# Splitting the weights of a two-layer trunk into high and low parts: units of 512 or of 1024 columns

## The chip, the cores and the metric

The kernel runs on one core of one Trainium2 chip. The metric is the device time of one execution in microseconds. The engines are named as in the profile: PE is the tensor engine's matrix product, PEld its weight load, DVE the vector engine, ACT the scalar engine, POOL the general engine, SP the engine that issues nearly all transfers. L55 is line 55 of the kernel before. The change keeps the line numbers, so L55 is the same statement in both.

## The reference

A trunk of two layers is applied to 288 tokens (256 of a prompt and 8 samples of 4) with 1024 features, all in float32. Each layer is

```python
h = h + 0.5 * swiglu(rmsnorm(h, ...), ffn1_gate_up, ffn1_down)
h = h + mixer(rmsnorm(h, ...))           # layer 0: Mamba-2, layer 1: RWKV-7
h = h + 0.5 * swiglu(rmsnorm(h, ...), ffn2_gate_up, ffn2_down)
h = h + (p[i] @ ple_in[i]) * sigmoid(rmsnorm(h, ...) @ ple_gate[i])
```

and a last norm follows. The feed-forward width is 22 x 128 = 2816. Besides the output, the mixers' new states are returned (the Mamba states and convolution rows, the RWKV states and shifted rows).

## The kernel before, in words

Features lie on the 128 partitions and the 288 tokens are the columns, so that a product takes a weight tile of 128 x 128 as the stationary operand and an activation tile of 128 x 288 as the moving one. The stages follow one another in this order: feed-forward, Mamba, feed-forward, the part with p ("ple"), feed-forward, RWKV, feed-forward, ple, final norm.

**Precision.** Most products are made in float32r, a format that the tensor engine takes in one pass. To keep float32's accuracy a weight w is split into a rounded high part and the exact rest, and so is the activation x; `mm3` (L144 to L149) then adds three products into one bank: high x high (L147), high x low (L148) and low x high (L149).

**The stream of weights.** `Stream` (L26) holds the tiles in the order of use: 3016 tiles in 377 units of UT = 8 tiles. `load` (L37 to L42) issues one transfer of 512 KB for a unit on SP's queue, into one of four raw buffers. `ahead` (L44 to L59) splits pieces of PT tiles: ACT copies the piece to a float32r buffer `whi` (L55), then DVE subtracts that from the raw piece into `wlo` (L56). `next` (L61) returns the two parts of the next tile, after it has called `ahead` with `la_split` = 16 tiles and `la_units` = 4 units:

```python
while self.split < min(self.n, self.used + tiles_split):
    ...
    src = self.raw[self.split // UT][:, (self.split % UT) * P:(self.split % UT + PT) * P]
    hi = self.k.wsp.tile([P, PT * P], F32R, tag="whi", name=f"whi{i}")
    lo = self.k.wsp.tile([P, PT * P], F32R, tag="wlo", name=f"wlo{i}")
    nc.scalar.activation(hi, src, AF.Copy)
    nc.vector.tensor_tensor(lo, src, hi.bitcast(F32), ALU.subtract)
    ...
    self.split += PT
```

The pool `wsp` (L1682) has eight buffers of each of `whi` and `wlo`, of 4 tiles each: 32 tiles. A buffer can be written again when the products of all its tiles have been made. A raw buffer can be loaded again when all of its tiles have been split. Part of RWKV's weights (88 tiles, the stream `wn`) is used whole, in float32, and is never split.

**What sets the order.** Each engine works through its own queue in order, and an instruction that waits holds up all that stand behind it on that engine. The program is written in Python without an explicit order for the queues: a planner (the tile framework's scheduler) places the instructions on each engine by the order in which the program makes them, by their readiness and by its own estimates of how long each takes. So the splits stand in ACT's and DVE's queues among the other work of those engines, at places that the planner chose:

- in a feed-forward part (`ffn_in`, L299) the gates' evacuation and the split of the hidden values; at its end `h_done` (L343), which makes the next operand from h and adds to the next norm's sum;
- in Mamba (`mamba`, L838) the split operands for the first projections (L853 and the lines after it), the convolutions (L671), the step sizes, the states;
- in RWKV (`rwkv`) the mixed operands (`mix`, L1100), the short products and copies of the recurrence for each pair of heads (`prep`, `chain`), and at the end the products with w_o, whose last operand hangs on the last pair's group norm;
- in the prologue (L424 to L434) the first operands, made tile by tile with calls of `ahead(min(PT * k, la_split), la_units)` between them, then the squares for the first norm.

The products themselves stand in PE's queue in an order that the planner chose likewise.

Of the kernel before, what the change touches and what calls it, by code (L numbers as in the profile page):

```python
# [19 lines left out]
UT = 8  # L20
PT = 4
# [4 lines left out]
class Stream:  # L26
    """Weight tiles [128, 128] in the order of use: loaded in units of UT tiles, split in
    pieces of PT tiles into a float32r high part and the exact float32r rest, or left whole."""
# [40 lines left out]
    def next_whole(self, name, kt, mt):  # L69
        """The next tile as float32, for a product in the tensor engine's own four passes."""  # L70
        self.order.append((name, kt, mt))
        while self.loaded < min(self.n, self.used + 2 * UT):
            self.load()
        u, o = divmod(self.used, UT)
        self.used += 1
        return self.raw[u][:, o * P:(o + 1) * P]


class K:
# [44 lines left out]
    def after(self, later, earlier):  # L124
        """Queue later behind earlier on their engine."""
# [3 lines left out]
    def act(self, out, in_, func, bias=None, scale=None):  # L129
        """An activation. Those of one table set stay together in the engine's queue, behind the set's load."""  # L130
# [20 lines left out]
    def hilo(self, hi, lo, src, scale=None):  # L151
        """hi = float32r(src * scale), lo = src * scale - hi, exactly."""
# [19 lines left out]
    def rsqrt(self, out, ps, eps, shift_eps=True, n=NT, y=None):  # L172
        """out = 1/sqrt(ps + eps): exp(-ln/2), then a Newton step."""
# [10 lines left out]
    def rstd(self):  # L184
        """The mean square's matrix product and the reciprocal root, on all partitions."""
# [23 lines left out]
    def renew(self, lo, hi, dt=F32R):  # L209
        """The shared tiles lo to hi anew, for values of type dt."""  # L210
# [29 lines left out]
    def ffn(self, name, down_next, ple=None, early=None):  # L240
        """The feed-forward part, and the part with p where it comes next: its layer, what comes after,
        whether p's products were made early; the layer of p's products where they fill the wait for
        the next norm: they are kept in DRAM."""
# [38 lines left out]
    def p_load(self, i, tiles):  # L282
        """The split parts of p for layer i."""
# [15 lines left out]
    def ffn_in(self, name, down_next, mid=None):  # L299
        """h += 0.5 * swiglu(x): x's split parts are in xh, xl (without the row's 1/rms)."""  # L300
# [44 lines left out]
    def h_done(self, mo, g):  # L345
        """A tile of h is final: its part of the next norm's sum and of the next operand."""
        if g is not None:
            self.split_h(mo, g)
        self.stat_add(mo)
# [37 lines left out]
    def final_done(self, mo):  # L387
        """A tile of h is final: its part of the norm's sum, the tile times the norm's weights."""
# [9 lines left out]
    def final(self, pool):  # L398
        """The norm and the output with the tokens on the partitions; the last block ends with the samples."""
# [24 lines left out]
    def prologue(self, g):  # L424
        """The split parts of the first operand; products that bring the tensor engine to its full clock."""
# [53 lines left out]
class Mamba:  # L479
# [65 lines left out]
    # dt and everything that only hangs on it, for all heads  # L545
# [26 lines left out]
    def dt_tokens(self):  # L572
        """dt, dt*A and their sums with the tokens on the partitions; the samples' three times."""
# [45 lines left out]
    def bc(self, ps, h, cols):  # L619
        """The running sums of the pair of heads from h, on 64 partitions each."""  # L620
# [5 lines left out]
    def exps(self, g):  # L626
        """exp(a_i - a_j), 0 where j > i, for the group's four heads; exp(a_i) for its two pairs."""
# [18 lines left out]
    def conv(self, g, n, ct, ps, raw):  # L646
        """The conv's rows to keep, the conv itself (without silu); raw: ps lacks the row's 1/rms."""
# [34 lines left out]
    def silus(self, g, conv, z):  # L682
        """The silus of group g's conv channels and of the gates z."""
# [8 lines left out]
    def ssd(self, g):  # L692
# [5 lines left out]
        # token-major x and B  # L698
# [37 lines left out]
        # (C_i . B_j), masked  # L736
# [7 lines left out]
        # the prompt's states  # L744
# [66 lines left out]
    def norm_act(self, g):  # L811
        """w = 1/sqrt of the group's mean square / 2, and (2 w)^2."""
# [7 lines left out]
    def norm_dve(self, g):  # L820
        """A Newton step, -1/sqrt = (v (2 w)^2 - 3) w, and the next operand."""
# [15 lines left out]
def mamba(k, gain, g_next):  # L837
# [9 lines left out]
    with k.tc.tile_pool(name="mamba", bufs=1) as pool:  # L847
# [20 lines left out]
        def boundary(g):  # L868
            """Between the tiles of group g and those of the next; the exponentials of two groups at once."""
# [122 lines left out]
class Rwkv:  # L992
# [49 lines left out]
    def lead(self, g, r):  # L1042
        """u, the shifted difference, the mixed operands; the first halves of the small products."""
# [29 lines left out]
    def gates(self):  # L1073
        """The first half of the gate's small products."""
# [15 lines left out]
    def stack(self, out, src, rows, other):  # L1090
        """The split parts on two ranges of partitions."""
# [3 lines left out]
    def stacked(self, ps, w, x, n, rows, start=True):  # L1095
        """A product whose operand's parts are stacked on n partitions, the high ones on rows; w twice there."""
# [3 lines left out]
    def mix(self, i, kt, out):  # L1100
        """The mixed operand i: float32, or in split parts (of r and v; the second half of v's where xx was)."""
# [13 lines left out]
    def sigmoid(self, out, ps, bias):  # L1115
        """exp(-ln(1 + exp(-z))), z = ps + bias kept from where exp leaves ln's range (there it is under 1e-18)."""
# [6 lines left out]
    def proj(self, n, i, x, p):  # L1123
        """A projection k, v or r of a pair of heads."""
# [15 lines left out]
    def bulk(self, p):  # L1140
        """The projections of a pair of heads that prep needs: decay and a (small), k, r."""
# [17 lines left out]
    def bulk2(self, p):  # L1159
        """The others: g, v, and v by tokens."""  # L1160
# [437 lines left out]
def _tiles(w):  # L1598
    """[K, M] -> [kt, mt, 128, 128], zero-padded."""
    kt, mt = -(-w.shape[0] // P), -(-w.shape[1] // P)  # L1600
    if w.shape != (kt * P, mt * P):
        z = np.zeros((kt * P, mt * P), w.dtype)
        z[:w.shape[0], :w.shape[1]] = w
        w = z
# [140 lines left out]
```

## Time and profile before

| | |
|---|---|
| median of 3 runs (range) | 1566.1 us (1565.0 to 1567.6) |
| profiled execution: span from first to last instruction | 1563.5 us |
| profiled execution: its own time beside the span | none is listed; the runs' median is 2.6 us above the span |
| PE busy | 1547.2 us, 99% |
| PEld busy | 1435.2 us, 92% |
| DVE busy | 1102.7 us, 71% |
| ACT busy | 982.5 us, 63% |
| the high parts, L55 on ACT | 754 instructions of 128 x 512, 472.0 us |
| the low parts, L56 on DVE | 754 instructions of 128 x 512, 516.0 us |
| raw weights, L40 on SP | 377 transfers of 512 KB |
| mean granted clock of the tensor engine | 0.997 |

In a group's row the numbers behind the bar are its busy time in us and the mean of one instruction in ns; then comes the idle time of the engine ahead of it, with what ended most of that. A row of waits reads "engine, instruction <- what it waited for: us in all, times, longest". In a row of a timeline stand start, duration, engine, line, operation and operands. Matmuls overlap in the pipeline: the mean of one is longer than the time from one start to the next.

### The profile page before, as it was taken

What the parts mean: (1) busy time and instruction counts of PE and PEld (TensorE: products, weight loads), DVE (VectorE), ACT (ScalarE), POOL (GpSimd) and SP (SyncE); (2) the same over time, 40 slices, a digit from 0 to 9 for tenths busy, and PEclk for the clock granted to TensorE, in tenths of its full rate; (3) what the DMA queues carried; (4) which work ended last, traced back from release to release, by engine and by line L of the source; (5) the groups of instructions that cost most, each with busy time, mean ns of one, the idle gap of its engine ahead of it and who ended that gap; (6) DMA issues with size and microseconds to landing.
All of it is one profiled execution on the core that took longest, in us unless ns stands there. A gap on an engine that the chain in (4) does not pass through costs nothing. (4 is left out here: it accounts for less than half of the span.)

```text
span 1563.5 us, 35166 instructions
## 1 busy us (share of the span) xinstructions
PE 1547.2 (99%) x13954; PEld 1435.2 (92%) x13954; DVE 1102.7 (71%) x2321; ACT 982.5 (63%) x2241; POOL 46.9 (3%) x142
## 2 busy tenths in 40 slices
PE   9999999999999999999999999999999999999998
PEld 9999998998989999999999999677777778999997
DVE  7666678888888666656866655976666777766656
ACT  7555458999987555545755555776666755555545
POOL 0000002111100000000000000100000000000000
PEclk9999999999999999999999999999999999999999
DMA  7555564765765555555555555432221224555551
GB/s 250 163 164 170 166 197 141 251 203 200 246 208 184 178 163 167 170 162 164 169 172 165 163 169 169 147 97 70 71 78 50 62 60 133 185 162 168 169 165 58
DMA packets 75572, 243.44 MB, mean 156 GB/s; under 512 B 11728, under 2 KB 16976, under 8 KB 75408
## 3 DMA queue, kind: packets, MB, share of 16 engines
q1 hardware_dynamic: 75408, 241.21, 49.4%
q8 instruction: 109, 1.79, 0.5%
q14 instruction: 55, 0.45, 0.1%
HBM read 226.54 MB, written 14.64 MB: 154 GB/s over the span
## 5 line engine op out<-in xcount | busy, mean ns | idle before, releaser
L147 PE MATMUL bank<-act,whi 128*128 128x288 f32 x2760 | 825.6, 300 | 5.8 <-ACT act L138 4.2
L148 PE MATMUL bank<-act,whi 128*128 128x288 f32 x2760 | 819.0, 297 | 0.9 <-DVE act L156 0.7
L149 PE MATMUL bank<-act,wlo 128*128 128x288 f32 x2760 | 814.3, 295 | 0.1
L55 ACT ACTIVATE whi<-raw 128x512 fp32r<-128x512 f32 x754 | 472.0, 631 | 434.4 <-PE bank L148 421.1
L56 DVE TENSOR_TENSOR wlo<-raw,whi 128x512 fp32r<-128x512 f32 x754 | 516.0, 690 | 263.3 <-ACT whi L55 235.2
L148 PEld LDWEIGHTS bank<-act,whi 128*128 128x128 f32 x2760 | 521.4, 189 | 10.2 <-issue 4.2
L147 PEld LDWEIGHTS bank<-act,whi 128*128 128x128 f32 x2760 | 517.0, 188 | 14.7 <-ACT act L138 5.4
L149 PEld LDWEIGHTS bank<-act,wlo 128*128 128x128 f32 x2760 | 520.5, 189 | 3.7 <-issue 0.8
L147 PE MATMUL bank<-more,whi 128*128 128x288 f32 x192 | 56.7, 295 | 0.0
L148 PE MATMUL bank<-more,whi 128*128 128x288 f32 x192 | 56.4, 294 | 0.0
L149 PE MATMUL bank<-more,wlo 128*128 128x288 f32 x192 | 56.4, 294 | 0.0
L321 DVE TENSOR_TENSOR t<-bank,rstd 128x288 f32<-128x288 f32 x88 | 39.9, 457 | 22.9 <-PE bank L149 22.9
L324 DVE TENSOR_TENSOR u<-bank,s 128x288 f32<-128x288 f32 x88 | 39.8, 457 | 22.6 <-PE bank L149 22.6
L671 DVE SCALAR_TENSOR_TENSOR conv_a<-X,vec,conv_a 128x312 f32<-128x312 f32 x96 | 51.1, 536 | 2.6 <-ACT conv_a L138 2.2
L138 ACT ACTIVATE s<-t 128x288 f32<-128x288 f32 x104 | 45.8, 443 | 6.1 <-DVE t L366 3.5
L138 ACT ACTIVATE X<-bank 128x256 f32<-128x256 f32 (+2 forms) x98 | 30.7, 340 | 20.0 <-PE bank L1304 19.2
L1131 PE MATMUL bank<-act,raw 128*128 128x288 f32 x128 | 42.5, 439 | 0.0
L138 ACT ACTIVATE act<-h,vec 128x288 fp32r<-128x288 f32 (+1 forms) x71 | 37.1, 528 | 7.3 <-DMA h<-in_xT 2.7
L148 PEld LDWEIGHTS bank<-more,whi 128*128 128x128 f32 x192 | 36.3, 189 | 0.0
L149 PEld LDWEIGHTS bank<-more,wlo 128*128 128x128 f32 x192 | 36.2, 189 | 0.0
L147 PEld LDWEIGHTS bank<-more,whi 128*128 128x128 f32 x192 | 36.0, 187 | 0.0
L133 ACT ACT_TABLE_LOAD x25 | 32.1, 1283 | 1.1 <-PEq L1719 0.7
(381 smaller groups left out, 1732.1 us busy)
## 6 DMA issues: line engine op xcount, KB each, us to landing
raw<-in_w SPq DMA_DIRECT2D x377, 512.0 KB, 3.6
h0a<-in_ssm_a SPq DMA_DIRECT2D x16, 512.0 KB, 5.6
h0b<-in_ssm_b SPq DMA_DIRECT2D x16, 512.0 KB, 4.8
out_ssm_s<-h0b SPq DMA_DIRECT2D x16, 512.0 KB, 3.8
raw<-in_wn SPq DMA_DIRECT2D x11, 512.0 KB, 3.7
S<-in_wkv_in SPq DMA_DIRECT2D x8, 256.0 KB, 3.9
out_wkv_s<-S SPq DMA_DIRECT2D x8, 256.0 KB, 2.0
h<-in_xT SPq DMA_DIRECT2D x8, 144.0 KB, 4.3
```

The lines of the kernel that those rows point to most:

```text
L55: nc.scalar.activation(hi, src, AF.Copy)
L56: nc.vector.tensor_tensor(lo, src, hi.bitcast(F32), ALU.subtract)
L133: load = self.nc.scalar.preload_act_table_set(s)
L138: i = self.nc.scalar.activation(out, in_, func, **kw)
L147: nc.tensor.matmul(ps, wh, xh, start=start, stop=False)
L148: nc.tensor.matmul(ps, wh, xl, start=False, stop=False)
L149: nc.tensor.matmul(ps, wl, xh, start=False, stop=stop)
L321: nc.vector.tensor_tensor(t, pg, r, ALU.mult)
L324: nc.vector.tensor_tensor(u, pu, s, ALU.mult)
L671: nc.vector.scalar_tensor_tensor(a[:, :312], X[:, t:t + 312], k.g(f"conv_w{t}")[:, ct:ct + 1], a[:, :312], ALU.mult, ALU.add)
L1131: self.nc.tensor.matmul(ps, k.wn.next_whole("r_wk", kt, p), x[kt], start=kt == 0, stop=kt == KD - 1)
```

## The change

The weights are split eight tiles (1024 columns) at a time, and the pool has four buffers of each kind instead of eight, each twice as large. The bytes that the buffers take in all stay the same (32 tiles of high and 32 of low parts), as does the size of a load. A piece is now a whole unit. A product that needs any tile of a piece now waits for the split of all eight, and a buffer is free only when the products of all eight tiles have been made. In the prologue the calls of `ahead` ask for 8 and 16 tiles where they asked for 4, 8, 12 and 16. The diff also takes out docstrings and comments, which changes no instruction.

```diff
@@ -18,14 +18,14 @@
 KF = 22
 EPS = 1e-6
 UT = 8
-PT = 4
+PT = 8
 FIRST = 2
 WARM = 16
...
@@ -1679,7 +1679,7 @@
     with tc.tile_pool(name="const", bufs=1) as k.const, \
             tc.tile_pool(name="wraw", bufs=4) as k.wraw, \
-            tc.tile_pool(name="wsp", bufs=8) as k.wsp, \
+            tc.tile_pool(name="wsp", bufs=4) as k.wsp, \
             tc.tile_pool(name="work", bufs=2) as k.work, \
```

## The prediction

> **What bounds the kernel now.** I read the page's first part, then each engine's busy time by stage, the waits, and the timelines around PE's few idle gaps.
>
> ```profile
> span 1563.5 us, 35166 instructions
> PE 1547.2 (99%) x13954; PEld 1435.2 (92%) x13954; DVE 1102.7 (71%) x2321; ACT 982.5 (63%) x2241; POOL 46.9 (3%) x142
> 40.00:80.00 40.00, 40.00 (x305) 40.00 (x304) 25.42 (x44) 21.06 (x38) 0.00 (x0) 1.00 0.54 165
> 226.00:487.00 261.00, 260.28 (x2817) 237.04 (x2815) 228.96 (x521) 228.60 (x666) 38.56 (x108) 1.00 0.62 207
> 985.00:1313.00 328.00, 323.31 (x3908) 238.55 (x3907) 233.98 (x621) 207.09 (x560) 4.08 (x13) 0.99 0.26 78
> PE bank L147 <- ACT act L138: 4.2, 4, 1.7
> PE bank L147 <- ACT whi L55: 1.5, 2, 0.8
> ```
>
> The windows give span, then PE, weight load, DVE, ACT, POOL, the granted clock, DMA share and GB/s. TensorE (PE) is the bound: 305 products in 40 us of a feed-forward stage are 40/305 = 131 ns each, back to back, so a tile of three products takes 0.393 us, four tiles 1.57 us, eight 3.15 us. Mamba is 226 to 487, RWKV 985 to 1313. PE idles only 1563.5 - 1547.2 = 16.3 us, 1.5 of it for a weight split. PE's modelled ends can hide short stalls; in RWKV, where weight loads fill 238.55 of 328 us, more could be hidden.
>
> The two operations that are regrouped, with the rows from which a 1024-column one is priced:
>
> ```profile
> L55 ACT ACTIVATE whi<-raw 128x512 fp32r<-128x512 f32 x754 | 472.0, 631 | 434.4 <-PE bank L148 421.1
> L56 DVE TENSOR_TENSOR wlo<-raw,whi 128x512 fp32r<-128x512 f32 x754 | 516.0, 690 | 263.3 <-ACT whi L55 235.2
> L138 ACT ACTIVATE act<-u 128x288 fp32r<-128x288 f32 x64 | 28.1, 444 | 0.0
> L156 DVE TENSOR_TENSOR act<-u,act 128x288 fp32r<-128x288 f32 x64 | 28.6, 452 | 0.0
> 985.84 2.17 ACT L55 ACTIVATE whi<-raw 128x512 fp32r<-128x512 f32 x4
> 251.98 3.19 DVE L56 TENSOR_TENSOR wlo<-raw,whi 128x512 fp32r<-128x512 f32 x5
> ```
>
> **Price of a bigger split.** ACT: (631 - 444)/224 = 0.835 ns a column, so 631 + 512 x 0.835 = 1058 ns. DVE: (690 - 452)/224 = 1.0625 ns, so 690 + 544 = 1234 ns. Each of 377 units trades two splits for one, saving 377 x (1262 - 1058) = 77 us of ACT busy time and 377 x (1380 - 1234) = 55 us of DVE's. Part of that is overlap already: back to back, splits start every (2.17 - 0.63)/3 = 0.51 us on ACT and (3.19 - 0.69)/4 = 0.62 us on DVE, so a queue that is truly full gains some 0.09 us a unit on either. What gets longer is a split as an obstacle: +0.43 us on ACT, +0.54 us on DVE, and the low part is ready +0.97 us after the split begins.
>
> **Steady feed-forward (with the p parts, 1563.5 - 261 - 328 = 974 us): 0.** Both rings still hold 32 tiles. ACT sits idle 421.1 us until the last product that reads a buffer (PE bank L148) frees it, so the ring sets when a split runs. Before, a buffer of four tiles is free 28 tiles ahead of its next use: 28 x 0.393 = 11.0 us, minus 0.63 and 0.69 leaves 9.7 us. After, eight tiles are free 24 ahead: 9.4 - 1.06 - 1.23 = 7.1 us. That lead is the cover. In Mamba and RWKV the engines postpone splits, but tiles are used no faster. Without cover each of the 377 units would cost up to the 0.97 us. The loads on SP's queue keep order and size; a raw buffer is free about 1 us later, when its low part is done, and what stands behind its next load on SP (Mamba's states, outputs) moves by as much. Against that 1 us stand the 32 tiles, 12.6 us, of four raw buffers and this landing (count, size, us):
>
> ```profile
> raw<-in_w SPq DMA_DIRECT2D x377, 512.0 KB, 3.6
> ```
>
> **Prologue: +0.5.** The first split stands between the weights' landing and the first product, the second unit's between eight finished tiles and the next:
>
> ```profile
> 6.85 0.63 ACT L55 ACTIVATE whi<-raw 128x512 fp32r<-128x512 f32 x1 [0.44 <-DMA raw<-in_w]
> 7.53 0.40 PE L147 MATMUL bank<-act,whi 128*128 128x288 f32 x1 [0.70 <-ACT whi L55]
> 11.13 1.14 ACT L55 ACTIVATE whi<-raw 128x512 fp32r<-128x512 f32 x2
> 11.80 0.40 PE L147 MATMUL bank<-act,whi 128*128 128x288 f32 x1 [0.83 <-ACT whi L55]
> 12.97 0.67 PE L149 MATMUL bank<-act,wlo 128*128 128x288 f32 x3
> ```
>
> (Timelines: start, duration, engine, line, out<-in, count, idle time before and what ended it.) The delay at 7.53 is swallowed by the 0.83 us gap at 11.80; there the 1058 ns split ends 0.43 us later, and PE with it. The low part comes 0.97 us later, a further half microsecond if PE's queue has nothing else to do. Bounds: 0 (the second unit is put ahead of the squares before it) and +1.0. I take +0.5. The Trainium skill bears on this place (Perfetto Trace Analysis, Optimizing Scalar/DVE Operations): where these engines are not saturated but cause bubbles on others, breaking up instructions may let work finish sooner. The two gaps agree in kind, and by that rule, too, the prologue loses.
>
> **Start of Mamba: +0.7.** DVE works without a pause here and postpones the low parts; PE uses them almost at once:
>
> ```profile
> 231.53 0.62 ACT L55 ACTIVATE whi<-raw 128x512 fp32r<-128x512 f32 x1
> 246.82 1.27 DVE L56 TENSOR_TENSOR wlo<-raw,whi 128x512 fp32r<-128x512 f32 x2
> 247.71 0.29 PE L149 MATMUL bank<-act,wlo 128*128 128x288 f32 x1
> 235.37 0.40 PE L147 MATMUL bank<-act,whi 128*128 128x288 f32 x1 [0.34 <-ACT act L138]
> 236.15 0.40 PE L148 MATMUL bank<-act,whi 128*128 128x288 f32 x1 [0.38 <-DVE act L156]
> ```
>
> The split of 231.53 gets its low part at 246.82, ready near 247.5, as PE reaches it at 247.71. In one piece both halves are ready at 246.82 + 1.23 = 248.05, so PE waits about 0.35 us unless the planner gives it other work. As much again can come where a 1.23 us split stands ahead of the operand splits for which PE already waits at 235 and 236 (0.34 + 0.38). Bounds: -0.7 (those two waits vanish, since DVE has less to do) and +2.0 (0.54 us in front of four such operands). I take +0.7.
>
> **Start and end of RWKV: +0.7.**
>
> ```profile
> 1002.64 0.63 ACT L55 ACTIVATE whi<-raw 128x512 fp32r<-128x512 f32 x1 [1.33 <-PE bank L148]
> 1003.18 0.43 ACT L138 ACTIVATE t<-rs_y 128x288 f32<-128x288 f32 x1
> 1003.52 0.43 ACT L138 ACTIVATE act<-t 128x288 fp32r<-128x288 f32 x1
> 1003.99 0.40 PE L147 MATMUL bank<-act,whi 128*128 128x288 f32 x1 [0.86 <-ACT act L138]
> 1307.20 0.63 ACT L55 ACTIVATE whi<-raw 128x512 fp32r<-128x512 f32 x1 [0.86 <-PE bank L148]
> 1307.74 0.48 ACT L138 ACTIVATE s<-bank,lnb 128x288 f32<-128x288 f32 x1
> 1310.54 0.63 ACT L55 ACTIVATE whi<-raw 128x512 fp32r<-128x512 f32 x1 [0.43 <-PE bank L148]
> 1311.46 0.44 ACT L138 ACTIVATE act<-act 128x288 fp32r<-128x288 f32 x1 [0.29 <-DVE act L1479]
> 1311.96 1.06 PE L147 MATMUL bank<-act,whi 128*128 128x288 f32 x6 [1.32 <-ACT act L138]
> ```
>
> At 1002.64 ACT waits for a buffer, splits, and only then makes the operand for which PE has stopped; a 1.06 us split adds its 0.43 us to PE's 0.86. At 1307.20 and 1310.54 a split stands ahead of a step of the last chain (the group norm's logarithm L1472, then the operand of w_o); the first could add 0.43 us to the stall of 1.32, the second has 0.29 us of room. With a half fewer splits one obstacle may also go. Bounds: -2.2 (both stalls vanish) and +2.1 (a whole 1.06 us split moves ahead of each operand). I take +0.7.
>
> **Other stage boundaries: +0.2.** At the ends of feed-forward parts a split of 0.63 us stands ahead of the last operand on ACT:
>
> ```profile
> 737.73 0.63 ACT L55 ACTIVATE whi<-raw 128x512 fp32r<-128x512 f32 x1 [0.94 <-PE bank L148]
> 738.27 0.52 ACT L138 ACTIVATE act<-h,vec 128x288 fp32r<-128x288 f32 x1
> ```
>
> With eight tiles this split isn't due there (only every second one is), but the one before it is longer. Five such places at -0.2 to +0.4 give -1 to +2; I take +0.2.
>
> **Middle of RWKV and Mamba: 0.** In Mamba ACT is busy 228.60 of 261 us and DVE 228.96, yet PE's waits for a split, 1.5 us in the whole span, are the prologue's two gaps (0.70 + 0.83) alone. In RWKV's middle an ACT that waits for a buffer holds up the chain behind it, half as often but for a longer split; the cases below bound it.
>
> **Sum.** 0.5 + 0.7 + 0.7 + 0.2 = +2.1 us: span 1565.6. The profile lists no time of the execution besides the span; the runs' median, 1566.1, lies 2.6 above it, which I carry over: 1568.2, forecast 1568. A measurement of this kernel tells about 0.2%, 3.1 us, from no change, so this is "no change", leaning slower. All lower bounds together are -3.9 us, all upper ones +7.1; they will not all fall on one side, so half of each way from the forecast, 1565 to 1571, is this case's own range.
>
> **Rivals.**
>
> *Lighter engines free PE* (-4.5 us, near 1562). If RWKV's time hangs on ACT, its 52 splits from 1004 to 1311 become 26, with 26 x 0.2 = 5 us less ACT work and half the waits:
>
> ```profile
> L55 ACT ACTIVATE whi<-raw x52: 612/630/650, 1021.7 to 1310.5; 128x512 fp32r<-128x512 f32 x52
> ACT whi L55 <- PE bank L148: 27.3, 25, 2.8
> ```
>
> Halved, the chain behind ACT gains up to 27.3/2 = 13.6 us, of which PE could get a third, 4.5 us (the share is a guess). Against it: PE waited for ACT's operands only 4.2 us in the whole span. Chance 0.13. The same section of the Trainium skill says that grouping into larger operations can improve throughput if the engine is saturated; the trace agrees that Mamba comes near, with ACT at 228.60 of 261 us.
>
> *Slower: the longer split blocks RWKV's short chain* (+7 us, near 1573). Place: ACT's and DVE's queues between 1004 and 1311, where the recurrence's short steps stand in line and PE's order is fixed. 26 units, each in front of one chain step on each engine, would cost 26 x (0.43 + 0.54) = 25 us; the deciding point is whether more than an eighth of it (3.1 us) reaches PE. A quarter, 6.3 us beside the start's and end's 0.7, gives +7. For it: 25 waits for L148 show that ACT's queue really stands behind splits. Against: two old splits together cost more than one new, and PE has w_o and projection products to fill with, planned for that. The planner, which orders all queues by its own costs, may also shift work by as much. Chance 0.30. The rule of the Trainium skill on breaking up instructions, named at the prologue, would give this sign; no row of the trace before shows it inside RWKV.
>
> *The change doesn't do what it says*: the buffers are of the same bytes in all and no split is bigger than a loaded unit, so I see no way; it would read 1566 and sits in "no change".
>
> **Chances.** No change 0.57, faster 0.13, slower 0.30. A range for 8 in 10 leaves out the far half of the gains and of the slow tail: 1562 to 1575.
>
> **What would show it.** Right: 377 L55 of about 1058 ns (busy about 398 us) and 377 L56 of about 1234 ns (about 463); 305 products in 40 to 80; PE's gap near 11.80 grown by 0.43 us; waits for L56 or L55 on PE near 247 and 1003. Wrong: new waits of PE for wlo in mid-Mamba, or a RWKV stage (328 us) that moves by over 3 us either way.

## The result: slower by 0.9%, and the profile after

The changed kernel takes 1580.5 us (median of 4 runs, 1577.3 to 1585.5) against 1565.6 us for the kernel before; the ratio is 1.0093, with a 95% interval from 1.0072 to 1.0113. The profiled execution spans 1579.1 us, 15.6 more than before's 1563.5.

The page of the changed kernel, first part and costliest groups. The columns are those that the prediction explains.

```profile
span 1579.1 us, 34131 instructions
PE 1556.0 (99%) x13954; PEld 1442.2 (91%) x13954; DVE 1057.4 (67%) x1944; ACT 899.6 (57%) x1864; POOL 44.6 (3%) x142
...
L55 ACT ACTIVATE whi<-raw 128x1024 fp32r<-128x1024 f32 x377 | 399.6, 1060 | 474.2 <-issue 294.3
L56 DVE TENSOR_TENSOR wlo<-raw,whi 128x1024 fp32r<-128x1024 f32 x377 | 461.1, 1224 | 208.3 <-ACT whi L55 207.2
```

The change does what it says. ACT has 83 us less to do, DVE 45 us less. Nothing of this reaches the end.

Windows of the changed kernel: a steady feed-forward stretch, Mamba, RWKV with its neighbourhood, then RWKV from its first small product (L1097) to the product that waits for w_o's last operand, and three stretches at half clock.

```profile
40.00:80.00 40.00, 40.00 (x305) 40.00 (x304) 23.62 (x31) 17.42 (x26) 0.00 (x0) 1.00 0.54 168
226.00:489.00 263.00, 261.78 (x2829) 238.33 (x2827) 227.91 (x470) 223.08 (x611) 38.65 (x108) 1.00 0.62 209
985.00:1331.00 346.00, 336.07 (x3936) 249.26 (x3935) 237.92 (x609) 205.86 (x545) 3.90 (x17) 0.97 0.26 80
993.57:1325.13 331.56, 321.63 (x3879) 237.11 (x3877) 225.11 (x574) 196.66 (x516) 2.24 (x13) 0.98 0.24 74
999.86:1003.27 3.41, 3.41 (x13) 2.85 (x12) 3.41 (x10) 2.91 (x8) 0.00 (x0) 0.50 0.52 161
1027.17:1034.00 6.83, 6.83 (x63) 5.83 (x59) 2.94 (x6) 3.40 (x9) 0.00 (x0) 0.50 0.25 82
1320.71:1330.95 10.24, 6.43 (x25) 6.11 (x26) 6.21 (x16) 4.40 (x10) 0.00 (x0) 0.50 0.57 166
```

The same two views of the kernel before, which has only one such stretch inside RWKV:

```profile
991.20:1311.96 320.76, 316.24 (x3877) 233.20 (x3877) 226.93 (x600) 202.23 (x543) 4.08 (x13) 0.99 0.24 74
998.44:1001.86 3.42, 3.37 (x11) 2.76 (x10) 3.42 (x9) 2.77 (x8) 0.00 (x0) 0.50 0.17 69
```

The steady stretch still makes 305 products in 40 us. RWKV starts 993.57 - 991.20 = 2.4 us late. It takes 331.56 instead of 320.76 us to the last operand, 10.8 us more; PE's idle time in it goes from 320.76 - 316.24 = 4.5 to 331.56 - 321.63 = 9.9 us, and the granted clock, the number behind the five engines, from 0.99 to 0.98. Behind it the half clock lasts on to 1330.95.

How the end of RWKV looks on PE, before (timeline; the rows of the last pair's states, L1428, of its group norm, and of the first product that waits for it):

```profile
1303.48 0.33 PE L1428 MATMUL bank<-AR,S 64*64 64x64 f32 x4
...
1307.00 0.29 PE L1187 MATMUL bank<-cl,ones_m 128*128 128x288 f32 x1
...
1311.96 1.06 PE L147 MATMUL bank<-act,whi 128*128 128x288 f32 x6 [1.32 <-ACT act L138]
```

and after:

```profile
1317.28 0.33 PE L1428 MATMUL bank<-AR,S 64*64 64x64 f32 x4
1317.54 0.40 PE L147 MATMUL bank<-act,whi 128*128 128x288 f32 x1
...
1317.91 0.29 PE L149 MATMUL bank<-act,wlo 128*128 128x288 f32 x1
...
1318.74 0.40 PE L1187 MATMUL bank<-cl,center 128*128 128x288 f32 x1 [0.16 <-DVE cl L1462]
1319.70 0.40 PE L1186 MATMUL bank<-ch,ones_m 128*128 128x288 f32 x1 [0.56 <-ACT ch L138]
1320.85 0.61 PE L1187 MATMUL bank<-cl,ones_m 128*128 128x288 f32 x1 [0.75 <-DVE cl L1194]
1325.13 0.85 PE L147 MATMUL bank<-act,whi 128*128 128x288 f32 x2 [3.68 <-ACT act L138]
...
1327.22 0.44 PE L149 MATMUL bank<-act,wlo 128*128 128x288 f32 x1
1327.46 0.44 PE L147 MATMUL bank<-act,whi 128*128 128x288 f32 x1
...
1331.02 0.29 PE L147 MATMUL bank<-act,whi 128*128 128x288 f32 x1
1331.15 0.29 PE L148 MATMUL bank<-act,whi 128*128 128x288 f32 x1
```

From the last state to the operand it takes 1311.96 - 1303.48 = 8.5 us before and 7.9 us after: the group norm is not slower. Before, the planner had kept 44 of w_o's products for these 8.5 us (44 x 0.131 = 5.8 us), and PE idled 1.32. After, they stand ahead of the last states; three are left (1317.54 to 1317.91), and PE idles 0.16 + 0.56 + 0.75 + 3.68 = 5.2 us. Then it works at half clock: products start 0.24 us apart (1327.22, 1327.46) and again 0.13 apart from 1331.02.

So half clock costs a queue of such products (0.24 - 0.13)/0.24 = 0.45 of its length (an estimate from these two spacings). The busy stretches at half clock in addition to before's, 1027.17 to 1034.00 and 1325.13 to 1330.95, are 6.8 + 5.8 us and cost about 5.7 us (estimate). With 2.4 us before RWKV and 5.4 us more idle time in it that is 13.5 of the 15.6 us. The remaining 2.1 us are spread over RWKV. PE changes there 207 times in each direction between products of 288 columns and those of another width, instead of 188 (counted in the two traces by the operands' columns; the figures of 183 and 158 in the expectations below come from another count), and such a change is not free:

```profile
1021.21 0.29 PE L147 MATMUL bank<-act,whi 128*128 128x288 f32 x1
1021.34 0.29 PE L148 MATMUL bank<-act,whi 128*128 128x288 f32 x1
1021.56 0.34 PE L1304 MATMUL bank<-X,N 64*64 64x64 f16 x10
1021.83 0.40 PE L149 MATMUL bank<-act,wlo 128*128 128x288 f32 x1
1022.07 0.29 PE L147 MATMUL bank<-act,whi 128*128 128x288 f32 x1
```

In the changed kernel the product before the small ones occupies 0.22 us (1021.34 to 1021.56) and the first behind them 0.24 (1021.83 to 1022.07), where 0.13 is usual. That such changes make up the 2.1 us isn't shown.

The programs differ far more than the diff. The planner has moved 3,198 of the 12,300 matrix instructions that the program makes to another place in TensorE's queue, up to 193 places off: 2,921 from RWKV on and 277 ahead of it. In ScalarE's queue 659 of 1,487 instructions beside the splits are moved, in VectorE's 562 of 1,567. The experiments ask whether this order, or the long splits and big buffers as the chip runs them, is the cause.

### The profile page after: what moved, and what is told of

Same layout as the page of the kernel before. It is cut to its first block, busy times and chain, and to the rows that moved or that the text cites. A ratio compares the mean times of both kernels' runs of the same rounds, so it can differ in the third digit from the quotient of the medians.

```text
span 1579.1 us, 34131 instructions
## 1 busy us (share of the span) xinstructions
PE 1556.0 (99%) x13954; PEld 1442.2 (91%) x13954; DVE 1057.4 (67%) x1944; ACT 899.6 (57%) x1864; POOL 44.6 (3%) x142
## 4 chain that ended last, share of the span: by engine, by line
PE 95%; DMA 2%; DVE 1%; ACT 1%; issue 0%; SPq 0%; POOL 0%; DVEq 0%; POOLq 0%; ACTq 0%
PE bank L147 26%; PE bank L148 25%; PE bank L149 25%; PE bank L1131 2%; PE bank L1304 2%; PE bank L1265 1%; PE bank L1442 1%; PE bank L770 1%; PE bank L766 1%; PE bank L774 1%; PE bank L641 1%; PE bank L1404 1%; PE bank L1081 1%; PE bank L1416 1%; PE bank L1186 1%; PE bank L747 0%
## 5 line engine op out<-in xcount | busy, mean ns | idle before, releaser
L55 ACT ACTIVATE whi<-raw 128x1024 fp32r<-128x1024 f32 x377 | 399.6, 1060 | 474.2 <-issue 294.3
L56 DVE TENSOR_TENSOR wlo<-raw,whi 128x1024 fp32r<-128x1024 f32 x377 | 461.1, 1224 | 208.3 <-ACT whi L55 207.2
L159 DVE SCALAR_TENSOR_TENSOR act<-h,vec,act 128x288 fp32r<-128x288 f32 x56 | 28.2, 513 | 13.3 <-ACT act L138 13.1
```

Of the source, the lines that this page charges most:

```text
L159: nc.vector.scalar_tensor_tensor(lo, src, scale, hi.bitcast(F32), ALU.mult, ALU.subtract)
```

## The experiments

Theory A: the planner's new order costs the time. B: the long instruction stands in the way at run time. C: the bigger buffers come free too late. D came up after the first runs: any new order costs. "RWKV" is the length of the stretch shown above (331.6 us for the changed kernel, 320.8 before) in the profiled execution. The runs of one kernel differ by the granted clock: the changed kernel's four take 1577.3 us at a mean clock of 0.995, 1579.9 and 1581.0 at 0.992, 1585.5 at 0.988. The profiled execution is one of these runs and not always near the median: in e8, e13 and e15 it is 4 to 5 us above it, in e9 it is the fastest, 10 us below.

| run | splits, buffers | order of the queues | median us | ratio (95%) | RWKV us |
|---|---|---|---|---|---|
| changed kernel | 1024, 4 big | own | 1580.5 | 1.0093 (1.0072 to 1.0113) | 331.6 |
| e1 | 1024, 4 big | PE as before in RWKV | 1594.9 | 1.0180 (1.0165 to 1.0196) | 346.4 |
| e2 | 512, 8 small | PE as after in RWKV | 1584.7 | 1.0124 (1.0109 to 1.0139) | 336.7 |
| e3 | 512 in RWKV, 4 big | own | 1579.7 | 1.0088 (1.0061 to 1.0116) | 331.1 |
| e4 | 512 outside, 4 big | own | 1580.2 | 1.0091 (1.0059 to 1.0122) | 336.6 |
| e5 | 512, 4 big | own | 1575.5 | 1.0058 (1.0042 to 1.0075) | 332.8 |
| e6 | as before, rate 1.6 | own | 1577.9 | 1.0070 (1.0047 to 1.0092) | 330.8 |
| e7 | as after, rate 1.25 | own | 1590.9 | 1.0148 (1.0111 to 1.0184) | 339.9 |
| e8 | as after, 28 extra products | own | 1576.6 | 1.0063 (1.0039 to 1.0088) | 331.0 |
| e9 | 1024, 4 big | all as before | 1589.9 | 1.0172 (1.0148 to 1.0195) | 326.5 |
| e10 | 512 in pairs, 4 big | all as before | 1582.2 | 1.0113 (1.0095 to 1.0131) | 327.1 |
| e11 | 512 in pairs, 8 small | all as before | 1577.6 | 1.0081 (1.0065 to 1.0097) | 322.0 |
| e12 | as after, rate 1.6 | own | 1587.7 | 1.0142 (1.0124 to 1.0160) | 334.8 |
| e13 | as before, 6 extra copies | own | 1570.5 | 1.0035 (1.0023 to 1.0046) | 325.8 |
| e14 | as before, 12 extra products | as before | 1564.5 | 0.9995 (0.9986 to 1.0004) | 320.4 |
| e15 | as before, rate 1.5 | own | 1565.5 | 1.0003 (0.9994 to 1.0012) | 322.9 |
| e16 | as after, EARLY 1 | own | 1580.9 | 1.0095 (1.0080 to 1.0109) | 330.8 |
| e17 | 512 in pairs, 4 big | all as after | 1581.3 | 1.0102 (1.0068 to 1.0136) | 333.9 |
| e18 | 512 in pairs, 8 small | all as after | 1580.2 | 1.0094 (1.0079 to 1.0109) | 333.2 |

### TensorE's order alone: e1, e2

The instructions of TensorE are recorded as they are made, and in RWKV each is made to follow the one that precedes it in the other kernel's queue:

```diff
...
+    q = [made[FROM + i + x] for i, x in enumerate(d)]
+    for a, b in zip(q, q[1:]):
+        tc.add_manual_dep(b, a.name, mybir.DependencyInfo(
+            mybir.DependencyClass.NoSync, mybir.DependencyReason.DATA), reason="order")
```

> The changed kernel (1024-column splits, four buffers), with TensorE's 3,630 instructions of RWKV held in the order that they have in the kernel before (158 changes in each direction between 288-column products and small ones, where the changed kernel's own order has 183). Theory A, the planner's new order on TensorE costs the time: 1566 to 1570 us, the RWKV stage within 4 us of the 323.7 us of before, and one clock drop of 3.4 us at RWKV's start at most. Theory B, the longer split itself costs it, by standing ahead of the recurrence's steps on ACT and DVE while the chip runs: 1577 to 1582 us, RWKV near 336 us. Between the two, 1571 to 1576, both have a share.

> The reverse: the kernel before (512-column splits, eight buffers), with TensorE's instructions of RWKV held in the order of the changed kernel. Theory A (order): 1574 to 1580 us, the clock drops near 1027 and 1320 us are there. Theory B (length of the split at run time): 1564 to 1568 us, as before.

Both are slower than either theory forecast, 1594.9 and 1584.7 us, and slower than the changed kernel, e2 only just (its interval begins at 1.0109, the changed kernel's ends at 1.0113). The planner orders ScalarE and VectorE anew around a fixed TensorE: besides the splits, 393 of ScalarE's 1,487 places and 394 of VectorE's 1,567 hold an instruction of another kind in e1 than in the kernel whose order TensorE has, and 420 and 391 in e2 (counted in the traces by line and tiles). That the three queues then no longer fit each other is the likely reason; it isn't shown. The two runs therefore say nothing on A against B; e9 to e11, e17 and e18 hold all three.

### Where the length matters: e3, e4, e5

The big buffers stay, but are filled by two splits on each engine, in RWKV (e3), outside it (e4), or everywhere (e5). The diff is condensed:

```diff
...
+            n = 4 if 2192 <= self.split < 2432 or self.split % 8 else 8   # e3; e4 the reverse; e5: n = 4
+            c = slice((self.split % PT) * P, (self.split % PT + n) * P)
+            nc.scalar.activation(hi[:, c], src, AF.Copy)
+            nc.vector.tensor_tensor(lo[:, c], src, hi[:, c].bitcast(F32), ALU.subtract)
+            self.split += n
```

> The changed kernel, its 1024-column buffers kept, but in RWKV (tiles 2192 to 2431) each buffer is filled by two 512-column splits on each engine. TensorE's order, which the planner makes, is then nearly that of before (161 changes each way). If the loss sits in RWKV and hangs on the split's length there (A and B alike): 1566 to 1570 us. If it hangs on the coarser release of the bigger buffers (theory C): 1577 to 1582 us.

> The complement: whole 1024-column splits in RWKV only, two 512-column ones into the same buffers everywhere else. If the loss sits in RWKV: 1576 to 1581 us, up to 2 us under the changed kernel for what prologue and Mamba give back. If it sits outside: 1566 to 1569 us.

> The changed kernel's four buffers of 1024 columns, each filled by two 512-column splits on each engine, everywhere: only the size of the buffers differs from the kernel before, no instruction is longer. Theory C, the coarser release of the buffers (a buffer comes free 24 tiles ahead of its next use instead of 28) costs the time, in RWKV: 1572 to 1582 us. Theories A and B (the longer instructions, by the planner's order or at run time): 1564 to 1568 us.

1579.7, 1580.2 and 1575.5 us. By these expectations e4 puts the loss into RWKV, e3 and e5 on the buffers (C). But in e5, too, the planner has reordered TensorE's queue: 2,309 of its places hold an instruction of another kind than before (line and tiles, counted in the traces; 3,256 in the changed kernel), so C and A are not apart yet. What e5 does show is that no instruction need be longer for 0.6% to go.

### A new order without any change of the splits: e6, e15, and the changed kernel's e7, e12

The share of fill work for each step of RWKV's recurrence is changed:

```diff
-RATE = 1.45
+RATE = 1.6   # e6 (kernel before), e12 (changed kernel); 1.5 in e15 (before), 1.25 in e7 (changed)
```

> The kernel before (512 columns, eight buffers) with 1.6 in place of 1.45 as the share of fill work to each step of RWKV's chain. TensorE's order then has 172 changes in each direction instead of 158, and is otherwise near that of before. Theory D, the time hangs on TensorE's order in RWKV as such, whatever made it, through spans of little TensorE work at which the granted clock drops: 1570 to 1580 us with more half-clock spans between 1000 and 1320 us than the one of before. If the order matters little without the bigger splits: 1564 to 1568 us.

> The changed kernel with 1.25 in place of 1.45. TensorE's order then has 169 changes in each direction instead of 183. Theory D: part of the loss comes back, 1570 to 1577 us, and the half-clock spans near 1027 and 1320 us move or vanish. Theory B or C: the loss stays, 1577 to 1582 us.

> The changed kernel with 1.6 in place of 1.45 as the share of fill work; TensorE's order has 172 changes in each direction instead of 183 and comes by its own way through RWKV. Theory D says that the time is drawn anew with each order: anywhere from 1568 to 1592 us, the half-clock spans at other places than 1027 and 1320 us. Theories B and C: 1577 to 1583 us, as the changed kernel.

> The kernel before with 1.5 in place of 1.45 as the share of fill work: splits and buffers unchanged, 1,810 of TensorE's instructions in RWKV at other places in its queue (the change moves 2,921, the kernel before with 1.6 moves 2,682 and takes 1577.9 us). Theory D, a new order costs whatever made it: 1569 to 1578 us. If small moves are free: 1564 to 1567 us.

1577.9, 1590.9, 1587.7 and 1565.5 us. Moving 2,682 of TensorE's instructions (e6) costs 12 us with the splits untouched, nearly what the change costs. Moving 1,810 of them (e15) costs nothing that can be told from noise, so D in its plain form, that any new order costs, is wrong. e15's new order is a mild one, though: counted by line and tiles, 260 places of TensorE's queue hold an instruction of another kind than before, against 2,290 in e6. The changed kernel found no better order at either rate; e7 missed the ranges of all theories, and e12 those of B and C.

### The stall and the half clock: e8, e13, e14, e16

In e8 the changed kernel gets 28 products in the last pair's group norm, into a bank that is free there; their result is not used.

```diff
+        def warm(n, x):
+            for _ in range(n if p == KD - 1 else 0):
+                nc.tensor.matmul(pz[:, :NT], self.ones_m, x, start=True, stop=True)
         self.mm2(pc, self.center, yh, yl)
+        warm(4, yl)
         self.mm2(pm, self.ones_m, sh, sl)
+        warm(24, sl)
```

> The changed kernel with extra products (28 of 288 columns, their result is not used) on TensorE in the group norm of RWKV's last pair, 4 in the gap near 1320.7 us and 24 in the gap of 3.68 us near 1321.5. If the half clock from 1320.71 to 1330.95 us follows from TensorE standing idle: that span vanishes or shrinks to 3.4 us, and the time falls by 2 to 4 us to 1576 to 1578. If the half clock comes from something else: the span stays, and the time is 1579 to 1583 us.

1576.6 us, 3.9 under the changed kernel. The two intervals overlap (1.0039 to 1.0088, and 1.0072 to 1.0113), so the times alone don't show the gain. The timeline of e8 and its window there:

```profile
1324.51 3.33 PE L1459 MATMUL bank<-cl,ones_m 128*128 128x288 f32 x24
1328.35 0.80 PE L147 MATMUL bank<-act,whi 128*128 128x288 f32 x4 [0.51 <-ACT act L138]
...
1328.99 0.29 PE L148 MATMUL bank<-act,whi 128*128 128x288 f32 x1
1329.12 0.29 PE L149 MATMUL bank<-act,wlo 128*128 128x288 f32 x1
```

```profile
1320.90:1331.10 10.20, 8.75 (x59) 7.59 (x56) 6.14 (x15) 5.40 (x12) 0.00 (x0) 1.00 0.41 122
```

The half clock is gone here and products start 0.13 us apart at once. The operand for which PE waits comes from ScalarE's and VectorE's chain, to which nothing was done: from the group norm's logarithm on it takes 3.64 us in both kernels (1321.49 to 1325.13 after, 1324.71 to 1328.35 in e8). So half clock there follows from PE's idling, and by the estimate above it costs 5.8 x 0.45 = 2.6 us. The runs bear this out: the mean clock of e8's six is 0.993 to 0.998, in the median 0.995, and that of the changed kernel's four 0.988 to 0.995, in the median 0.992. The profiled execution itself is the slowest of the six, 1581.8 us; it has half clock at Mamba's start, from 238.54 to 241.96 and in this window, where the changed kernel's has none and the edit changes nothing:

```profile
248.78:255.61 6.83, 6.83 (x30) 6.38 (x29) 5.42 (x12) 5.39 (x15) 1.53 (x1) 0.50 0.34 86
```

In e13 the kernel before gets the stall that it lacks:

```diff
         k.act(rs, rs, AF.Exp, scale=-0.5)
+        for _ in range(6 if p == KD - 1 else 0):
+            k.act(rs, rs, AF.Copy)
```

> The kernel before with six extra copies on ScalarE (288 columns, 0.43 us each, in place, they change nothing) in the group norm of RWKV's last pair, so that TensorE's gap near 1310.6 us grows from 1.3 to about 3.9 us; the rest of its order stays. If a stall costs only its own length: 1568 us. If the half clock follows it, as in the changed kernel near 1320 us (3.4 to 10.2 us at half clock): 1570 to 1573 us.

1570.5 us, 5.5 more (3.6 to 7.2 by the interval). The timeline and a window:

```profile
1319.46 0.53 PE L147 MATMUL bank<-act,whi 128*128 128x288 f32 x2 [4.34 <-ACT act L138]
...
1321.59 0.44 PE L147 MATMUL bank<-act,whi 128*128 128x288 f32 x1
1321.83 0.44 PE L148 MATMUL bank<-act,whi 128*128 128x288 f32 x1
```

```profile
1320.25:1323.66 3.41, 3.41 (x16) 3.41 (x16) 2.89 (x7) 2.55 (x7) 0.00 (x0) 0.50 0.91 265
```

PE's gap grows from 1.32 to 4.34 us, 3.0 us, and 3.41 us at half clock come behind it, 3.41 x 0.45 = 1.5 us: 4.5 of the 5.5. A stall costs more than its length here. The profiled execution is one of the two slowest of eight (1574.7 us) and has more half clock elsewhere, so the two terms are set against the median and not against its own time.

In e14 the gap at RWKV's start, which both kernels have, is filled in the kernel before:

```diff
                 k.mm3(ps, k.ws.next("r_w" + n, kt, p), x[kt], kt == 0, kt == KD - 1)
+            if (n, p, kt) == ("r", 0, 0):
+                pw = k.bank("A")[:, :NT]
+                for _ in range(12):
+                    self.nc.tensor.matmul(pw, self.ones_m, x[0][1], start=True, stop=True)
+                k.ring_at["A"] = 0
```

> The kernel before with 12 extra products of 288 columns (1.57 us, their result is not used) in TensorE's gap of 1.67 us near 994.4 us, its order otherwise the same. If the half clock from 998.44 to 1001.86 us follows from little TensorE work in the 3.4 us before it: that span is gone and the time falls by about 1.7 us to 1563.5 to 1564.5. If it has another cause: the span stays, 1565 to 1566.5 us.

1564.5 us, a ratio of 0.9995 with an interval across 1. The timeline and window of e14:

```profile
993.15 1.76 PE L1137 MATMUL bank<-act,ones_m 128*128 128x288 f32 x12
```

```profile
997.80:1001.20 3.40, 3.06 (x16) 2.17 (x15) 3.40 (x10) 2.55 (x7) 0.00 (x0) 1.00 0.02 7
```

The half clock at RWKV's start is gone, and the median of the mean clock over all runs is 0.998 instead of 0.997, so PE's idling is the cause here too. What that gives (1.5 us by the estimate above) is too little for this measurement. PE waits there for ScalarE's operands anyway.

In e16 the changed kernel keeps more of w_o's products for the end:

```diff
-EARLY = 3
+EARLY = 1
```

> The changed kernel with EARLY = 1 in place of 3: twelve tiles of w_o's products are kept for RWKV's end, about seven of them behind the last states in the planned order, 2.8 us of work for TensorE's stall of 3.68 us near 1321.5. If the stall and the half clock behind it cost about 6 us there: 1573 to 1577 us, and no half-clock span near 1320. If the work is only moved: 1579 to 1582 us.

1580.9 us: no gain. The timeline of e16 shows why:

```profile
1319.52 0.40 PE L1187 MATMUL bank<-cl,ones_m 128*128 128x288 f32 x1 [0.27 <-DVE cl L1194]
1323.72 0.85 PE L147 MATMUL bank<-act,whi 128*128 128x288 f32 x2 [3.80 <-ACT act L138]
```

Of w_o's products 17 now stand between the last state and the stalled product (counted in the trace; 3 in the changed kernel, 44 in the kernel before). They fill the small gaps, of which 0.27 us is left, but none of them stands behind the last L1187, and the large gap is still 3.80 us, with 6.83 us at half clock behind it. The planner decides where kept work goes.

### All three queues held: e9, e10, e11 in the old order, e17, e18 in the new

Every instruction of TensorE, ScalarE and VectorE is held in one kernel's order, in the whole program. Only the splits differ. In the old order a long split stands at the place of the second of the two short ones, and in e10 and e11 both short ones stand there; in the new order two short ones stand where the long one did.

```diff
...
+    for e, z in ORDER.items():          # PE, Activation, DVE
...
+        q = [MADE[e][i] for i in struct.unpack("<%dh" % (len(d) // 2), d)]
+        for a, b in zip(q, q[1:]):
+            tc.add_manual_dep(b, a.name, ...)
```

> The changed kernel (1024-column splits, four buffers) with TensorE, ScalarE and VectorE all held in the order of the kernel before, in the whole program; each long split stands at the place of the second of the two short ones that it replaces. If the planner's reordering costs the time (theory D): 1564 to 1570 us, as before. If the longer split or the coarser buffers cost it on the chip whatever the order (B, C): 1575 to 1590 us, and TensorE waits for splits or for chain steps in RWKV.

> As the long one in the old order, but each 1024-column buffer is filled by two 512-column splits side by side at that place: the same order, the same buffers, short instructions. If the length of the instruction matters at run time (B): 5 us or more under its long twin. If only buffers or order matter: within 2 us of it. Theory D: 1564 to 1570 us.

> The kernel before (512-column splits, eight buffers) in its own order on the three engines, but with the splits moved together in pairs, the first to the place of the second, as the twin with the big buffers has them. Theory D: 1564 to 1568 us. If the big buffers' late release costs time (C), this one is at before's time and the twin with big buffers is 5 us or more above it. If splitting later in pairs costs the time by itself, both are above 1570.

> The changed kernel's own order on TensorE, ScalarE and VectorE in the whole program and its four big buffers, but each long split is two 512-column ones side by side at its place. If the order makes the time: 1578 to 1583 us with the half-clock spans near 1027 and 1320 us, as the changed kernel. If the length of the instruction makes it: 1565 to 1572 us. ScalarE has 77 and VectorE 55 us more to do than with the long ones (by the mean durations), so a loss of some us against the changed kernel, to 1583 to 1588, would say that the long split is by itself a gain.

> As that, with the eight buffers of 512 columns of the kernel before: nothing of the change is left but the order of the three engines' queues. If the order makes the time: 1577 to 1583 us, with both half-clock spans. If the buffers' late release makes it: 1565 to 1570 us.

In the old order every step costs: short splits in pairs 1577.6 us (+13.0 on that chip's 1564.6), big buffers 1582.2 (+4.6), long splits 1589.9 (+7.7; its runs go from 1580.0 us at a clock of 0.997 to 1594.7 at 0.984). Most of the loss of the pairs lies in Mamba, not in RWKV, which takes 322.0 us. The timeline and a window of e11 (all lines read L1693, the recording one):

```profile
244.27 0.40 PE L1693 MATMUL bank<-act,wlo 128*128 128x288 f32 x1 [2.45 <-DVE wlo L1693]
```

```profile
245.13:258.78 13.65, 13.65 (x57) 11.67 (x56) 6.68 (x20) 6.06 (x17) 0.33 (x2) 0.50 0.29 84
```

At Mamba's start the first half of a unit now comes too late, PE waits 2.45 us for it, and 13.65 us at half clock follow. So the old order doesn't fit splits that come later. Held in it, the long splits and big buffers cost 25 us, more than the 15 of the planner's new order. A long split at the place of the first of the two short ones was not run.

In the new order the length and the buffers make no difference that can be told from noise: 1580.2 us with short splits and small buffers (e18), 1581.3 with big buffers (e17), 1580.5 with long splits, within each other's intervals. e18 has nothing of the change but the order of the queues, in which the splits come in pairs, and its ratio, 1.0094, is the change's 1.0093. In its trace and e17's, the three queues run through the same operations and tiles as the changed kernel's, place by place, apart from the splits. e18's windows and timeline show the changed kernel's RWKV nearly again:

```profile
991.66:1324.88 333.22, 324.18 (x3878) 239.05 (x3876) 227.15 (x602) 200.05 (x543) 4.50 (x13) 0.97 0.23 73
996.24:1003.06 6.82, 6.25 (x20) 5.35 (x21) 6.71 (x16) 4.90 (x13) 0.81 (x1) 0.50 0.41 144
1006.48:1013.30 6.82, 6.66 (x14) 4.68 (x15) 4.56 (x14) 1.14 (x4) 0.00 (x0) 0.50 0.00 0
1320.50:1330.74 10.24, 6.46 (x25) 6.14 (x26) 6.21 (x16) 4.92 (x11) 0.00 (x0) 0.50 0.56 166
```

```profile
1324.88 1.10 PE L1693 MATMUL bank<-act,whi 128*128 128x288 f32 x3 [3.68 <-ACT act L1693]
```

The same stall of 3.68 us, the same 10.24 us at half clock behind 1320, and RWKV at 333.2 us; it begins at 991.66, only 0.5 us later than before. The half clock near 1027, which was expected of e17 and e18, is in neither profile. Theirs stands near 996, 1006 and 1112 instead, so the places of the early half clock are not fixed by the order alone.

That the splits come in pairs is not what costs here: in the old order (e11) the pairs cost 10.9 us ahead of RWKV and 1.2 in it, in e18 0.5 us and 12.5.

Theory A holds: the new order alone makes the loss. B and C fall as direct causes in that order; they work through the planner, which answers to longer splits or bigger buffers (e5) with another order. In the old order they do cost, 7.7 and 4.6 us, so the old order would not have saved the change. That no better order exists for the long splits isn't shown. Nor is why the planner's estimates chose this one. No version ran faster than the kernel before beyond its interval.

## Why the prediction was wrong

**Sizes of the splits: right.** 377 high parts of 1060 ns (1058 forecast), 399.6 us in all (398); 377 low parts of 1224 ns (1234), 461.1 us (463).

**Steady feed-forward, 0: right.** 305 products in 40 us. Counted by the place in PE's queue, the changed kernel is the same 1.1 us behind from 32 us to 230 us, and about 1.6 us behind from 490 to 950.

**Prologue, +0.5: low, and just over its upper bound of 1.0.** The changed kernel's timeline at the rows of the prediction:

```profile
8.35 0.40 PE L147 MATMUL bank<-act,whi 128*128 128x288 f32 x1 [0.84 <-ACT whi L55]
...
12.53 0.40 PE L147 MATMUL bank<-act,whi 128*128 128x288 f32 x1 [0.51 <-ACT whi L55]
...
14.25 0.80 PE L149 MATMUL bank<-act,wlo 128*128 128x288 f32 x4 [0.40 <-DVE wlo L56]
```

The second unit's first product starts 0.73 us later (12.53 against 11.80). With the 0.40 us for the low part the prologue comes to 1.1. The sign that I named, a gap at 11.80 grown by 0.43 us, did not come: the gap is 0.51 instead of 0.83 us, since the delay arose at 8.35 already. In the six other profiles of kernels with this prologue (e1, e3, e7, e8, e12, e16) the delay at 71 us goes from 0.4 to 1.3 us, so the forecast has the right size and this execution lies high.

**Start of Mamba, +0.7: right at its place, but not kept; other boundaries, +0.2: too low.** With the prologue I had 1.4 us, and RWKV begins 2.4 us late. That this is near is partly luck. The delay grows by 0.7 us to 1.8 near 240, as forecast, but is 0.8 at 448, so Mamba has given back more than its start cost. Its end then adds 0.9, and the entry of RWKV 0.8, where PE waits 1.35 us for an operand (982.69) and did not wait before. The wait for a low part came, but at 239.21 and not near 247:

```profile
239.21 0.40 PE L149 MATMUL bank<-act,wlo 128*128 128x288 f32 x1 [0.47 <-DVE wlo L56]
```

```profile
982.69 1.48 PE L1052 MATMUL bank<-act,raw 128*128 128x288 f32 x5 [1.35 <-ACT pin L138]
...
1006.26 0.40 PE L147 MATMUL bank<-act,whi 128*128 128x288 f32 x1 [1.35 <-ACT act L138]
```

**Start and end of RWKV, +0.7 (bounds -2.2 and +2.1): the step that failed first.** At the start the working was right: the stall of 0.86 us became 1.35 (1006.26 above), +0.49 where I had +0.43; with a short split at that place (e18) it is 0.92. At the end I let the split in front of the group norm's logarithm add 0.43 us to a stall of 1.32 in an otherwise unchanged queue. The queue changed: the products that had filled the last 8.5 us were gone, and the stall became 3.68 us, with 1.5 us in three smaller ones ahead of it.

**Middle of RWKV and Mamba, 0: wrong for RWKV.** The step assumed that PE's order stays. RWKV to its last operand takes 10.8 us more, well over the 3 us that I had named as a sign of being wrong. Of this the middle has the half clock from 1027.17 to 1034.00, about 3.1 us by the estimate, and some 2 us that are spread. e18, with the splits as they were before in size, has the same changes between products of 288 columns and others and loses 12.5 us, with the early half clock at other places.

**The granted clock had no term.** The row for RWKV before said 0.99, and I didn't ask what stood behind it: 3.4 us at half clock behind a gap of 1.67 us (e14). Half clock is about 5.7 of the 15.6 us. The runs spread over 8 us with the clock (1577.3 us at 0.995 to 1585.5 at 0.988), and the range of 13 us, made of stalls alone, had no term for that.

**The rivals.** The slower one had the sign and the place, at +7 us and 0.30. Its mechanism, long splits in front of single steps of the recurrence, is not what happened: in the new order the length costs nothing (e17, e18). Its last sentence, that the planner may shift work by as much, was the cause, and it had no price of its own; e6 shows that a constant of the schedule alone moves the kernel before by 12 us. The rule of the Trainium skill on breaking up instructions (Perfetto Trace Analysis, Optimizing Scalar/DVE Operations) gave the right sign; inside RWKV the runs don't bear out its reason, since breaking them up again in that order (e17) gained nothing that can be told from noise. "Lighter engines free PE" fell: ACT and DVE have 128 us less to do, and PE waits more.

## What to carry to other kernels

Where a planner orders the queues, an edit has to be priced by the new order and not by the edited instructions alone: compare the queues of the two programs before any sum is made, and take the spread that a neighbouring constant of the schedule gives (here 0 to 12 us) as a first size of that term. To tell an order from the work, hold the queues of all compute engines in one order and change the work alone, once in each order, since the two answers can differ; holding one engine only mixes both. Where TensorE is the bound, look at what fills the last chain's latency, and price a stall with the half clock behind it.

## What the runs showed of the hardware

The clock falls for stretches of 3.41 us or multiples of it (3.41, 6.83, 10.24, 13.65 us in the traces here), with products of 288 columns 240 instead of 131 ns apart. A gap in PE's row isn't needed for it. The window of the changed kernel ahead of the drop at 1027.17:

```profile
1023.80:1027.20 3.40, 3.40 (x85) 2.47 (x86) 3.03 (x8) 1.99 (x7) 0.00 (x0) 1.00 0.51 154
```

PE counts as busy throughout, but with 85 instructions that stream some 3,360 columns by the trace, of which the steady stretch takes 305 x 288 x 3.41/40 = 7,490 in the same time. With each trace cut into windows of 3.41 us from its first drop on, 18 of the 25 drops inside the kernel over six traces (before, after, e1 to e4) follow windows among the fifth with the fewest columns of those in RWKV. But 98 of the 123 windows of that fifth are followed by no drop, and e18, with the same order of products, has none near 1027. So the exact condition stays open. The Trainium skill (TensorE: Matmul & The Clock Gate, Why this matters for your kernels) asks to avoid idle gaps above about 3 us between bursts; here the drop of 998.44 in the kernel before follows a gap of 1.67 us, and that at 1027.17 no gap at all.
